# Value products of a hybrid attention trunk: two banks of transposes per run on TensorE

## The chip, the cores and the metric

The kernel runs on one core of a Trainium2 chip. The metric is the device time of one execution in microseconds (us). Before the change the median of three runs is 3219.77 us (3219.07 to 3225.04). TensorE (PE) does the matmuls and the transposes, VectorE (DVE), ScalarE (ACT) and GpSimd (POOL) the elementwise work, and SyncE (SP) issues the DMAs.

## The reference

One layer over 2048 tokens of width 1024 in float32:

- `h = rmsnorm(x)`, and one projection `h @ w_in` that gives the queries, keys and values of four groups of four heads (64 wide): A stick-breaking attention, causal; B native sparse attention with three branches (compressed keys, eight selected blocks of 64 keys, a window of 512), summed by gates; C differential attention, two softmax maps per head, causal; D a window of 128 with sinks.
- Every branch ends in the same product, `o[q, d] = sum over k of P[q, k] * v[k, d]`, with `P` the weights of 128 queries over the keys that they may see, and `v` 64 wide.
- The groups' outputs are normalised, joined (`mix`), multiplied by `w_out` and added to `x`; then `x = x + relu(rmsnorm(x) @ w_up)^2 @ w_down` with a hidden width of 4096, and a last norm.

## The kernel before

**Stages.** The tokens are handled in four chunks of 512. The dense part runs in the order P0 to P3 (projections), then M0 to M3 (`w_out` and the MLP of a chunk); its matmuls write PSUM tiles `pd`, named pdP and pdM in the profile. Each dense product is split into high and low halves of reduced float32, three matmuls for one (`w_hi`, `w_lo`, `T_hi`, `T_lo`, `u_hi`, `u_lo`). Attention runs beside it, chunk by chunk in the order A, C, D, B (`GROUPS`, L34), on blocks of 128 queries. M of a chunk needs the attention of that chunk, through `mix_d` in DRAM.

**One block of attention.** The scores of 128 queries are made on PE into PSUM tiles `z` (three), turned to weights by DVE and ACT in SBUF tiles `row` (seven), and queued by `item` (L873) as a list of blocks: 128 keys for two heads in A, B and D, two times 128 keys of one head in C. A block thus holds up to two 128x128 pieces, for the half `j = 0` and the half `j = 1` of the output.

**Values.** `values` (L878) takes the items in order. It goes over the blocks by two. For each two it transposes up to four pieces of 128x128 on PE (`tr`, profile line L294) into one PSUM bank of tag `t` (two of them), which ACT copies to an SBUF tile `PT` (three of them, `PB`). This is called a bank here. The products of a bank are made one bank later: when the transposes of the next bank have been written, `products` (L931) writes those of the bank before. If there is no further item, or no free `PT`, the pending bank's products are written at once. A product is `mm(o[64*j:64*j+64, 0:128], v, p)`: the 128x64 values are the weights that PE loads, the transposed piece is the moving operand, and the result goes to partitions 0 to 63 or 64 to 127 of the one PSUM tile `o`. All products of an item add up in the same `o`; at the end of the item it is copied out (`oS`). Each product of float32 operands shows as two MATMUL records, so a full bank has eight.

**Order.** The kernel writes its instructions in an order that it works out itself: `run` (L1483) polls ten generators, and each yields either None or a function (`when`) that tells at what modelled time its next PE instruction has its inputs. The first generator in the list whose time has come goes on; `values` stands ahead of `scores`, and `dense` last. The model charges a value product half of its 128 columns (`share=2`). Instructions reach an engine's queue through the tile framework, which is started with `schedule_with_timeline_sim=True` and can move instructions against each other where their data allows it; PE then takes its instructions in the order that results.

Of the kernel before, what the change touches and what calls it, by code (L numbers as in the profile page):

```python
# [30 lines left out]
UNITS = 4  # L31
QB, RB, PB, WB = 4, 7, 3, 3
PD, ZB, TB = 3, 2, 2
GROUPS = "ACDB"  # L34
OFF = S - 128
UO = 2 * (NT - 1)
# [160 lines left out]
class Trunk:  # L197
# [631 lines left out]
    def loads(self):  # L829
        for c in range(NC):  # L830
            for g in GROUPS:
                yield from getattr(self, "loads_" + g)(c, 4 * c, max(0, c - 1))
# [43 lines left out]
        self.vq.append((self.pa, blocks, v, o, fin, first, last, rel))  # L876

    def values(self):  # L878
        prev = None
        while True:  # L880
            while not self.vq:
                if prev:
                    yield from self.products(*prev)
                    prev = None
                    continue
                if "scores" in self.over:
                    self.over.add("values")
                    return
                yield None
            pa, blocks, keys, obox, fin, first, last, rel = self.vq.pop(0)  # L890
            vt = []
            for k in keys:
                while isinstance(k, tuple) and k not in self.kq:
                    if prev:
                        yield from self.products(*prev)
                        prev = None
                    yield None
                vt.append(self.kq[k] if isinstance(k, tuple) else k)
            blocks = blocks(*vt)
            nb = len(blocks)  # L900
            end = [max(b for b in range(nb) if len(blocks[b][0]) > j) if len(blocks[0][0]) > j else -1
                   for j in range(2)]
            for g in range(0, nb, 2):
                bl = blocks[g:g + 2]
                if self.res["PT"].free == 0 and prev:
                    yield from self.products(*prev)
                    prev = None
                yield from self.res["PT"].take()
                yield self.when([p for P, _ in bl for p in P], "t", TB)
                self.pa = pa  # L910
                ps = self.tt()
                pt = self.tile(self.at, [128, 4, 128], F32, "PT", PB)
                n = 0
                for a, (P, _) in enumerate(bl):
                    for j in range(len(P)):
                        self.tr(ps[:, 2 * a + j, :], P[j])
                        n = 2 * a + j + 1
                self.evac(pt[:, :n], ps[:, :n])
                fl = g + 2 >= nb
                if fl and rel:  # L920
                    rel()
                ops = []
                for a, (P, v) in enumerate(bl):
                    for j in range(len(P)):
                        ops.append((j, v[j], pt[:, 2 * a + j, :], first and g + a == 0, last and g + a == end[j]))
                new = (pa, obox, pt, ops, first and g == 0, fin if fl else None)
                if prev:
                    yield from self.products(*prev)
                prev = new

    def products(self, pa, obox, pt, ops, first, fin):  # L931
        yield self.when([pt] + [v for _, v, _, _, _ in ops], "o" if first else None, 1)
        self.pa = pa
        if first:
            obox.append(self.ot())
        o = obox[0]
        for j, v, p, st, sp in ops:
            self.mm(o[64 * j:64 * j + 64, 0:128], v, p, st, sp, share=2)
        self.res["PT"].give()
        if fin:  # L940
            yield from fin(o)

# [30 lines left out]
    def scores(self):  # L973
# [4 lines left out]
        for c in range(NC):  # L978
            for g in GROUPS:
                if g == "D":  # L980
# [587 lines left out]
```

## Time and profile before

| | us |
|---|---|
| median of three runs | 3219.77 |
| profiled execution | 3224.61 |
| span of the profiled execution | 3222.9 |
| PE busy | 3128.8 (97%) |
| DVE busy | 2063.7 (64%) |
| ACT busy | 1776.0 (55%) |

The span reaches from the first to the last instruction; the profiled execution's own time is 1.7 us longer. A time of the timeline is counted from the start of the span. Busy time of PE is the union of its instructions' recorded durations; matmuls overlap in the array, so that the recorded duration of one (0.40 us for 128x512) is longer than the step from one start to the next (0.23 us).

### The profile page before, as it was taken

The numbers are of one execution on the slowest core, as the hardware profiler recorded it, in microseconds if no ns is written. First come the engines' busy times: TensorE is split into PE (matmuls) and PEld (weight loads), VectorE is DVE, ScalarE is ACT, GpSimd is POOL, SyncE is SP. The second block draws the span as 40 slices with busy tenths as digits, with TensorE's granted clock in tenths as the row PEclk, the third lists the DMA queues.
The fourth block names the chain that finished last, engine by engine and source line by source line (L and its number), as shares of the span: only waits on it lengthen the run. The fifth ranks groups of instructions, "written<-read, shape, count | busy, mean of one in ns | idle before, by whom it ended". The sixth has DMA issues, their size and how long they took to land.

```text
span 3222.9 us, 51242 instructions
## 1 busy us (share of the span) xinstructions
PE 3128.8 (97%) x19152; PEld 2510.3 (78%) x19152; DVE 2063.7 (64%) x4278; ACT 1776.0 (55%) x3459; POOL 714.2 (22%) x479
## 2 busy tenths in 40 slices
PE   7999999999999999999999999999999999999998
PEld 6887877878877777778877677778777777888886
DVE  4774668645668877666658887777655554545545
ACT  4764667545667755555657775565555543333333
POOL 3042312323212122232211122233212112310000
PEclk9999999999999999999999999999999999999999
DMA  7777555664133343364232333444522222423332
GB/s 213 193 193 206 160 160 148 191 176 134 57 97 87 100 110 105 97 164 121 61 100 68 99 95 88 110 117 134 141 63 83 65 61 74 149 81 97 92 98 85
DMA packets 456649, 376.53 MB, mean 117 GB/s; under 512 B 127056, under 2 KB 405712, under 8 KB 454736
## 3 DMA queue, kind: packets, MB, share of 16 engines
q1 hardware_dynamic: 456400, 373.26, 42.0%
q8 instruction: 151, 2.47, 0.3%
q14 instruction: 98, 0.80, 0.1%
HBM read 319.59 MB, written 53.58 MB: 116 GB/s over the span
## 4 chain that ended last, share of the span: by engine, by line
PE 77%; DVE 9%; ACT 5%; DMA 4%; issue 2%; SPq 1%; POOL 1%; DVEq 0%; POOLq 0%; ACTq 0%
PE pdM L290 43%; PE pdP L290 11%; DVE row L116 7%; PE tB L294 4%; PE oB L290 4%; PE zB L290 4%; ACT row L116 4%; PE oC L290 2%; PE zC L290 2%; PE tC L294 2%; SPq L246 1%; PE oA L290 1%; DVE acc L116 1%; PE tA L294 1%; PE zA L290 1%
## 5 line engine op out<-in xcount | busy, mean ns | idle before, releaser
L116 POOL TENSOR_TENSOR w_lo<-raw,w_hi 128x1024 fp32r<-128x1024 f32 (+1 forms) x188 | 469.4, 2501 | 1248.9 <-ACT w_hi L116 1105.4
L116 ACT ACTIVATE w_hi<-raw 128x1024 fp32r<-128x1024 f32 (+2 forms) x376 | 388.2, 1047 | 499.4 <-PE pdM L290 309.5
L116 DVE TENSOR_TENSOR acc<-acc,pdM 128x512 f32<-128x512 f32 (+1 forms) x576 | 370.3, 654 | 193.5 <-PE pdM L290 182.0
L290 PE MATMUL pdM<-T_lo,w_hi 128*128 128x512 f32 (+1 forms) x1088 | 419.6, 386 | 4.4 <-POOL T_lo L116 4.4
L290 PE MATMUL pdM<-T_hi,w_hi 128*128 128x512 f32 (+1 forms) x1088 | 419.5, 387 | 3.8 <-DVE nx L116 2.2
L290 PE MATMUL pdM<-T_hi,w_lo 128*128 128x512 f32 (+1 forms) x1088 | 420.8, 387 | 0.0
L290 PE MATMUL pdM<-w_hi,u_hi 128*128 128x512 f32 x1024 | 405.5, 403 | 11.6 <-DVE acc L116 8.4
L290 PE MATMUL pdM<-w_hi,u_lo 128*128 128x512 f32 x1024 | 405.2, 396 | 3.9 <-DVE u_lo L116 3.9
L290 PE MATMUL pdM<-w_lo,u_hi 128*128 128x512 f32 x1024 | 404.7, 396 | 0.0
L116 DVE TENSOR_TENSOR w_lo<-raw,w_hi 128x1024 fp32r<-128x1024 f32 (+1 forms) x188 | 241.2, 1290 | 214.5 <-ACT w_hi L116 206.0
L116 ACT ACTIVATE row<-row 128x1024 f32<-128x1024 f32 (+7 forms) x292 | 229.0, 801 | 118.5 <-DVE row L116 115.8
L290 PEld LDWEIGHTS pdM<-T_lo,w_hi 128*128 128x128 f32 x1088 | 206.5, 190 | 45.9 <-POOL T_lo L116 4.9
L290 PEld LDWEIGHTS pdM<-T_hi,w_hi 128*128 128x128 f32 x1088 | 206.0, 190 | 45.3 <-DVE nx L116 2.5
L116 ACT ACTIVATE PT<-tB 128x512 f32<-128x512 f32 (+1 forms) x260 | 135.9, 532 | 189.4 <-PE tB L294 186.7
L290 PEld LDWEIGHTS pdM<-T_hi,w_lo 128*128 128x128 f32 x1088 | 206.4, 190 | 42.1 <-issue 1.0
L290 PEld LDWEIGHTS pdM<-w_hi,u_hi 128*128 128x128 f32 x1024 | 193.2, 189 | 58.0 <-DVE acc L116 13.2
L290 PEld LDWEIGHTS pdM<-w_hi,u_lo 128*128 128x128 f32 x1024 | 193.7, 189 | 42.7 <-DVE u_lo L116 5.3
L290 PEld LDWEIGHTS pdM<-w_lo,u_hi 128*128 128x128 f32 x1024 | 193.6, 189 | 41.4 <-issue 1.2
L116 ACT ACTIVATE row<-row,c_mn 128x1024 f32<-128x1024 f32 (+4 forms) x192 | 171.6, 896 | 85.6 <-DVE c_mn L116 84.4
L290 PE MATMUL pdP<-T_hi,w_lo 128*128 128x512 f32 x480 | 194.1, 404 | 3.7 <-DVE w_lo L116 3.7
L290 PE MATMUL pdP<-T_lo,w_hi 128*128 128x512 f32 x480 | 193.4, 403 | 0.0
L290 PE MATMUL pdP<-T_hi,w_hi 128*128 128x512 f32 x480 | 192.7, 401 | 0.0
(209 smaller groups left out, 6604.8 us busy)
## 6 DMA issues: line engine op xcount, KB each, us to landing
raw<-in_w_up_dram SPq DMA_DIRECT2D x128, 512.0 KB, 4.1
raw<-in_w_down_dram SPq DMA_DIRECT2D x128, 512.0 KB, 3.6
raw<-in_w_in_dram SPq DMA_DIRECT2D x72, 512.0 KB, 4.9
acc<-in_x_dram SPq DMA_DIRECT2D x32, 512.0 KB, 4.3
raw<-in_w_out_dram SPq DMA_DIRECT2D x32, 512.0 KB, 4.4
qst<-qk_qA SPq DMA_DIRECT2D x64, 128.0 KB, 3.5
qst<-qk_qC SPq DMA_DIRECT2D x128, 64.0 KB, 2.6
qst<-qk_qD SPq DMA_DIRECT2D x64, 128.0 KB, 3.4
```

The source lines that it names most:

```text
L116: return f(*a, **k)
L246: self.nc.sync.dma_start(dst, src)
L290: self.nc.tensor.matmul(out, a, b, start=start, stop=stop, **k)
L294: self.nc.tensor.transpose(out, a, self.ident[:a.shape[0], :a.shape[0]])
```

## The change

`values` collects up to two pending banks of the same item in a list (`run`) and hands the list to `products` when the transposes of a third bank have been written, when the item ends and the next item's first transposes have been written, or when there is nothing else to do. `products` then writes the products of all banks in the list one after the other, with one `when` ahead of them that asks for all their inputs. The list is gone through backwards: the bank transposed last comes first. The flags for the first and the last matmul of a sum are set for the run as a whole. The number of transposes, copies and products stays as it is.

```diff
+RUN = 2
...
     def values(self):
-        prev = None
+        run = []
...
-                new = (pa, obox, pt, ops, first and g == 0, fin if fl else None)
-                if prev:
-                    yield from self.products(*prev)
-                prev = new
-
-    def products(self, pa, obox, pt, ops, first, fin):
-        yield self.when([pt] + [v for _, v, _, _, _ in ops], "o" if first else None, 1)
+                if run and (len(run) == RUN or run[-1][-2]):
+                    yield from self.products(run)
+                run.append((pa, obox, pt, ops, first and g == 0, fl, fin if fl else None))
+
+    def products(self, run):
+
+        pa, obox, _, _, first, _, _ = run[0]
+        yield self.when([x for r in run for x in [r[2]] + [v for _, v, _, _, _ in r[3]]], "o" if first else None, 1)
         self.pa = pa
         if first:
             obox.append(self.ot())
         o = obox[0]
-        for j, v, p, st, sp in ops:
-            self.mm(o[64 * j:64 * j + 64, 0:128], v, p, st, sp, share=2)
-        self.res["PT"].give()
+
+        ops = [x for r in run[::-1] for x in r[3]]
+        of = [[n for n, x in enumerate(ops) if x[0] == j] for j in range(2)]
+        starts = [n[0] if any(ops[i][3] for i in n) else -1 for n in of]
+        stops = [n[-1] if any(ops[i][4] for i in n) else -1 for n in of]
+        for n, (j, v, p, _, _) in enumerate(ops):
+            self.mm(o[64 * j:64 * j + 64, 0:128], v, p, n == starts[j], n == stops[j], share=2)
+        self.res["PT"].give(len(run))
+        fin = run[-1][-1]
+        run.clear()
```

The other places that wrote the pending bank (`if prev: yield from self.products(*prev)`) now write the pending run in the same way.

## Rows read from the trace of the kernel before

**Rows 1.** The page's first part: busy time, share of the span and instructions of each engine; and the granted clock in 40 slices.

```profile
PE 3128.8 (97%) x19152; PEld 2510.3 (78%) x19152; DVE 2063.7 (64%) x4278; ACT 1776.0 (55%) x3459; POOL 714.2 (22%) x479
PEclk9999999999999999999999999999999999999999
```

**Rows 2.** Busy time by stretch: stretch, its length, then busy us and count of instructions of PE, PEld, DVE, ACT and POOL, the granted clock, the DMA share and GB/s.

```profile
0.00:100.00 100.00, 82.49 (x469) 71.41 (x470) 49.68 (x99) 48.47 (x93) 28.47 (x51) 0.98 0.73 214
...
1800.00:1900.00 100.00, 95.51 (x566) 72.40 (x567) 86.47 (x96) 77.65 (x123) 14.05 (x6) 0.98 0.29 76
...
2500.00:2600.00 100.00, 100.00 (x614) 77.94 (x612) 57.84 (x127) 52.19 (x99) 17.27 (x8) 1.00 0.20 60
```

**Rows 3.** The chain of waits at its end, merged: start, duration, what it was.

```profile
2706.24 66.86 PE pdM L290 x290
...
2863.62 345.87 PE pdM L290 x1523
```

**Rows 4.** Groups of instructions of PE by line, operation, tile and form: count, busy us and mean ns of one, then the idle time ahead of them and what ended it. The value products.

```profile
L290 PE MATMUL oB<-PT,v 128*64 128x128 f32 x1648 | 137.6, 285 | 0.0
L290 PE MATMUL oC<-PT,v 128*64 128x128 f32 x1088 | 99.4, 289 | 0.2 <-ACT PT L116 0.2
L290 PE MATMUL oA<-PT,v 128*64 128x128 f32 x1088 | 93.2, 287 | 1.8 <-ACT PT L116 1.7
L290 PE MATMUL oD<-PT,v 128*64 128x128 f32 x248 | 22.0, 286 | 0.0
L290 PE MATMUL oB<-PT,vcn 128*64 128x128 f32 x128 | 16.2, 298 | 0.0
```

**Rows 5.** The timeline of PE around a run of one bank between dense matmuls: start, duration, instruction and count.

```profile
2046.48 0.40 PE L290 MATMUL pdM<-T_lo,w_hi 128*128 128x512 f32 x1
2046.71 0.39 PE L290 MATMUL pdM<-T_hi,w_lo 128*128 128x512 f32 x1
2047.04 0.66 PE L290 MATMUL oC<-PT,v 128*64 128x128 f32 x8
2047.62 0.50 PE L290 MATMUL pdM<-T_hi,w_hi 128*128 128x512 f32 x1
2047.96 0.39 PE L290 MATMUL pdM<-T_lo,w_hi 128*128 128x512 f32 x1
```

**Rows 6.** The same around two banks whose products happen to stand one behind the other.

```profile
1151.20 0.39 PE L290 MATMUL pdM<-w_lo,u_hi 128*128 128x512 f32 x1
1151.52 1.09 PE L290 MATMUL oC<-PT,v 128*64 128x128 f32 x16
1152.54 0.50 PE L290 MATMUL pdM<-w_hi,u_hi 128*128 128x512 f32 x1
1152.87 0.40 PE L290 MATMUL pdM<-w_hi,u_lo 128*128 128x512 f32 x1
```

**Rows 7.** The timeline of PE where transposes and products take turns.

```profile
1673.59 1.09 PE L290 MATMUL oB<-PT,v 128*64 128x128 f32 x16
1674.61 0.66 PE L294 MATMUL tB<-ident,row 128*128 128x128 f32 x4
1675.20 0.66 PE L290 MATMUL oB<-PT,v 128*64 128x128 f32 x8
1675.78 0.66 PE L294 MATMUL tB<-ident,row 128*128 128x128 f32 x4
```

**Rows 8.** The timeline of PE around eight transposes between dense matmuls.

```profile
1292.25 0.39 PE L290 MATMUL pdM<-T_lo,w_hi 128*128 128x512 f32 x1
1292.48 1.03 PE L294 MATMUL tC<-ident,row 128*128 128x128 f32 x8
1293.27 0.48 PE L290 MATMUL pdM<-T_hi,w_lo 128*128 128x512 f32 x1
1293.59 0.40 PE L290 MATMUL pdM<-T_hi,w_hi 128*128 128x512 f32 x1
```

**Rows 9.** The timeline of PE: the first and the last of the 587 stretches in which nothing but value products follow each other.

```profile
87.89 0.44 PE L290 MATMUL oA<-PT,v 128*64 128x128 f32 x4
...
2693.15 1.09 PE L290 MATMUL oB<-PT,v 128*64 128x128 f32 x16
```

**Rows 10.** Who waited for what, PE alone: total us, times, longest.

```profile
PE oA L290 <- ACT PT L116: 1.7, 5, 0.7
...
PE oC L290 <- ACT PT L116: 0.2, 1, 0.2
```

**Rows 11.** The timeline of all engines: a copy to PT, and the products that come after it.

```profile
1602.49 0.57 ACT L116 ACTIVATE PT<-tB 128x512 f32<-128x512 f32 x1
...
1605.11 0.66 PE L290 MATMUL oB<-PT,v 128*64 128x128 f32 x8
```

**Rows 12.** The timeline of PE where the products of one bank are not in one piece.

```profile
1128.23 0.43 PE L290 MATMUL oA<-PT,v 128*64 128x128 f32 x2
1128.74 0.50 PE L290 MATMUL zC<-kst,qst 128*128 128x512 f32 x1
1129.17 0.65 PE L290 MATMUL oA<-PT,v 128*64 128x128 f32 x6
```

**Rows 13.** Groups of instructions of ACT by form: the copies to PT of a full bank in A.

```profile
L116 ACT ACTIVATE PT<-tA 128x512 f32<-128x512 f32 x128 | 75.7, 596 | 11.8 <-PE tA L294 11.8
```

More of the change, by code (lines that the diff above doesn't have):

```diff
@@ L878, in values @@
     def values(self):
-        prev = None
+        run = []
         while True:
             while not self.vq:
-                if prev:
-                    yield from self.products(*prev)
-                    prev = None
+                if run:
+                    yield from self.products(run)
                     continue
@@ L893, in values @@
                 while isinstance(k, tuple) and k not in self.kq:
-                    if prev:
-                        yield from self.products(*prev)
-                        prev = None
+                    if run:
+                        yield from self.products(run)
                     yield None
@@ L904, in values @@
                 bl = blocks[g:g + 2]
-                if self.res["PT"].free == 0 and prev:
-                    yield from self.products(*prev)
-                    prev = None
+                if self.res["PT"].free == 0 and run:
+                    yield from self.products(run)
                 yield from self.res["PT"].take()
@@ L925, in values @@
                         ops.append((j, v[j], pt[:, 2 * a + j, :], first and g + a == 0, last and g + a == end[j]))
-                new = (pa, obox, pt, ops, first and g == 0, fin if fl else None)
-                if prev:
-                    yield from self.products(*prev)
-                prev = new
-    def products(self, pa, obox, pt, ops, first, fin):
-        yield self.when([pt] + [v for _, v, _, _, _ in ops], "o" if first else None, 1)
+                if run and (len(run) == RUN or run[-1][-2]):
+                    yield from self.products(run)
+                run.append((pa, obox, pt, ops, first and g == 0, fl, fin if fl else None))
+    def products(self, run):
+        pa, obox, _, _, first, _, _ = run[0]
+        yield self.when([x for r in run for x in [r[2]] + [v for _, v, _, _, _ in r[3]]], "o" if first else None, 1)
         self.pa = pa
```

## The prediction

> **What bounds the kernel now.** I read the page's first part, then the busy times by stretch, then who waited for whom, then the timeline of PE instruction by instruction. The first part [rows 1] says PE: 97% of the span, at a clock granted in full almost throughout, with DVE at 64% and ACT at 55%. The idle rest of PE is 3222.9 - 3128.8 = 94.1 us, of which 100 - 82.5 = 17.5 us fall into the first 100 us, before attention works [rows 2]. From there on PE idles in small pieces: nothing in 2500 to 2600 us, 4.5 us in 1800 to 1900 us, where DVE is at its fullest, 86% [rows 2]. Nor does the end of attention hold up the dense part: the last value product starts at 2693.15 us [rows 9], and the chain of waits shows dense matmuls of the chunk before still running from 2706.24 us for 66.9 us; the last uninterrupted stretch begins at 2863.62 us [rows 3]. So the time is the sum of what PE does, in whatever order, and an edit is worth what it takes off PE.
>
> A second look is needed at what "busy" hides. The groups of value products show no idle time ahead of them (0.0 to 1.8 us for over a thousand instructions each) and 368 us of busy time in all [rows 4], so by this view they cost what their number costs, and the change, which keeps the number, would save nothing. The starts in the timeline say otherwise. Dense matmuls of 512 columns start 0.23 us apart; but from the last one ahead of a run of products to the run it is 0.33 us, and from the first one behind it to the second 0.34 us [rows 5]. Each run of products thus delays its neighbours, and the recorded durations cover that up.
>
> The Trainium skill (Perfetto Trace Analysis, section Tensor Engine Instruction) says that the profiler takes the start of a PE instruction from the engine but computes the end from its size. By the busy rows the sum below would be zero, by the starts it is what follows; I go by the starts.
>
> **The change part by part.**
>
> *Fewer runs.* First the price of one run. From the dense matmul ahead of it to the second one behind it a run of eight takes 2047.96 - 2046.71 = 1.25 us [rows 5], one of sixteen, two banks that chance put side by side, 1152.87 - 1151.20 = 1.67 us [rows 6]. The eight more products add 0.42 us, and what is left of the first is 1.25 - 0.42 - 2 x 0.23 = 0.37 us: the price of beginning and ending a run among dense matmuls. Among transposes: four transposes and eight products take 1675.78 - 1674.61 = 1.17 us [rows 7]. Eight transposes among dense matmuls take 1293.59 - 1292.25 = 1.34 us, less two steps of 0.23 us 0.88 us, so 0.11 us each [rows 8]; four are 0.44 us. The price is 1.17 - 0.44 - 0.42 = 0.31 us. Of the 587 stretches in which the trace shows products alone [rows 9], I count 367 that are followed by a transpose. Weighted so, (367 x 0.31 + 220 x 0.37) / 587 = 0.33 us. All runs together cost about 194 us, 6% of the time.
>
> Then the number of runs. A bank is two blocks of an item, so the loops give it. A has two pairs of heads and 16 query blocks i of i + 1 blocks (from i = 8 on two items, the second of eight): 144 banks. C has four heads and half as many blocks: 160. B has 32 compressed items of one bank, 84 banks of windows and 144 of selected keys: 260. D has 32. That is 596, and 587 stretches fit it: some banks are joined by chance [rows 6], some are cut in two [rows 12]. In runs of two within an item A needs 80, C 96, B 32 + 56 + 80 = 168, D 32: 376, that is 220 fewer. Not all of these are a gain. In the trace 39 joined banks sit in stretches of more than eight; the new order would have joined most of them anyway, so 220 - 39 = 181 is the low end. The new order will also have chance neighbours, across items. I take 190, nearer the low end. 190 x 0.33 = 63 us. Both ends: 181 x 0.31 = 56 us and 220 x 0.37 = 81 us.
>
> *The bank transposed last comes first.* This costs no instruction. Its copy to PT takes 0.60 us [rows 13], and all products of the run now stand behind it. Before, between a bank's transposes and its products stood the run of the bank before and the next bank's transposes; now only the latter. The cover goes down by one run, 0.58 us [rows 5]. In the trace the cover is usually long: the copy that ends at 1602.49 + 0.57 = 1603.06 us is used at 1605.11 us, 2.05 us later [rows 11], and all waits of value products for a copy come to 1.7 + 0.2 = 1.9 us in 6 times [rows 10]. Bounds: 0 below, and above a whole copy for each of the 220 merged runs, 220 x 0.60 = 132 us. The rows are far nearer to 0; I take 0 here and let it stand as a rival.
>
> *Longer hold of buffers.* Two of three PT tiles are held until a run is over, so the copies of the next two banks wait for it; the two PSUM banks of tag t let a third bank's transposes go only when the first is copied. Dense matmuls and scores fill such time, and they have somewhere to go until 2773 us [rows 3]. If attention had no filler, each pair of banks would show some 0.5 us of idle PE; the rows give no sign of that, so 0, with the next item as the upper end.
>
> *What is late next.* When PE takes 2% less for the same work, DVE and ACT have 2% less time beside it. From 1800 to 1900 us DVE is at 86% and PE loses 4.5 us [rows 2]; there the saving may be eaten in part. The 64 merges in A, where this lies, are worth 64 x 0.33 = 21 us at most. I take off a third of that, 7 us, and nothing elsewhere.
>
> Sum: 63 - 7 = 56 us. The profiled execution took 3224.61 us, so 3168.6 us; it lies 4.84 us above the median of 3219.77 us, and the same subtraction there gives 3164 us, 1.7% less.
>
> **The rivals.**
>
> *Half is eaten.* PE takes its instructions in an order fixed beforehand. If the removed time is mostly where another engine is just in time, waits grow. For it: 94.1 us of PE idle are already there [rows 1], in over 30 kinds of waits. Against it: in stretches like 2500 to 2600 us PE doesn't idle at all, with DVE at 58% and ACT at 52% [rows 2]. With half of 63 us: 3219.8 - 31 = 3189 us.
>
> *The run waits for its first product (slower).* The place is the first matmul of each run, which asks for the copy made last. PE takes matmuls in order, so everything behind it waits as well, also dense matmuls that are ready. With a whole copy per merged run, 132 us less the 63 us: 3219.8 + 69 = 3289 us. It decides from 63 / 220 = 0.29 us of waiting per merged run. Against it: a cover of 2 us [rows 11] and 1.9 us of such waits in the whole trace [rows 10], where losing 0.58 us of cover turns few into waits.
>
> The Trainium skill (TensorE: Matmul & The Clock Gate, Part 3, section The mechanism) has matmuls start and end strictly in program order; only loads of weights are drawn ahead. That is the rule that speaks against putting the newest bank first; the trace of before agrees in so far as the products' few waits show as idle time of PE.
>
> *The runs don't come out whole.* The framework may put other matmuls between two products, as it did where a score cuts one bank's products into two and six [rows 12]. If most runs of sixteen were cut once, the number of stretches would stay near 587 and the time near 3220 us. Against it: 24 stretches of sixteen came out whole with no help, and banks cut like this are some 30 of 596.
>
> **How the numbers follow.** The sum as it stands: 0.68, with a range of its own of 3140 (nearly 81 us less) to 3178 us (42 us less). Half is eaten: 0.20. Runs cut: 0.07. Waits for the first product: 0.05. The range of 8 in 10 goes from 3142 us to 3198 us: it holds the first case but for its edges, and most of the second. Times within 0.2% (6.4 us, about what can be told from no change here) come from the runs that are cut: 0.06. Slower by more: the waiting rival and a remainder of the third, 0.05. Faster: 0.89.
>
> **What would show it.** Right: stretches of sixteen products dominate, each 1.02 us from its first start to the next instruction, and the number of stretches is near 400; counts of products and transposes stay as in rows 4; steps of 0.33 us ahead of products are fewer in the same proportion; PE's idle time grows by no more than some 10 us. Wrong: idle time of PE ahead of the o tiles put down to ACT's PT (the waiting rival: it would have to reach tens of us); 550 stretches or more (cut runs); idle time ahead of dense matmuls and scores put down to DVE and ACT that grows by 30 us (half eaten). The prediction fails as a whole if the price of a run is not for beginning and ending it but for each bank, against which the sixteen speak [rows 6].

## The result, and the profile after

The changed kernel takes 3187.41 us (median of five, 3182.32 to 3192.22) against 3219.63 us before: a ratio of 0.9897, 95% interval 0.9882 to 0.9911, 32 us or 1.0% less. Forecast were 3164 us with 3142 to 3198 us as the range: the direction and the range held, the gain is a little over half of the 56 us.

The two profiled executions lie at opposite ends of their runs (3224.61 us is near the highest of five before, 3225.04 us; 3182.32 us is the lowest after), so their traces differ by 42.3 us. The accounts below are of the traces; where two kernels are called faster or slower than each other, the medians say so.

One correction to the description ahead of the prediction: there are two PSUM tiles `z` for scores, not three (`ZB` is 2; the three is `PD`, the dense sums).

The first part of the page after the change (compare [rows 1]; span 3180.6 us):

```profile
PE 3074.8 (97%) x19152; PEld 2515.3 (79%) x19152; DVE 2068.3 (65%) x4278; ACT 1772.9 (56%) x3459; POOL 710.3 (22%) x479
PEclk9999999999999999999999999999999999999999
```

The counts are those of before on every engine. PE's busy time is 54.0 us less, and its idle time 3180.6 - 3074.8 = 105.8 us, 11.7 us more. The groups of value products, to set beside [rows 4]:

```profile
L291 PE MATMUL oB<-PT,v 128*64 128x128 f32 x1648 | 121.5, 281 | 0.0
L291 PE MATMUL oC<-PT,v 128*64 128x128 f32 x1088 | 87.2, 285 | 0.0
L291 PE MATMUL oA<-PT,v 128*64 128x128 f32 x1088 | 79.6, 282 | 1.7 <-DMA v<-nat_vA 1.7
L291 PE MATMUL oD<-PT,v 128*64 128x128 f32 x248 | 22.5, 287 | 0.0
```

As many instructions of nearly the same length, but A, B and C, whose banks were joined, are busy 42 us less together, while D, with one bank per item, is not. No product waits for ACT's PT any more. The timeline of PE where transposes and products take turns, as in [rows 7]:

```profile
1691.02 0.60 PE L295 MATMUL tB<-ident,row 128*128 128x128 f32 x4
1691.55 1.09 PE L291 MATMUL oB<-PT,v 128*64 128x128 f32 x16
1692.57 0.66 PE L295 MATMUL tB<-ident,row 128*128 128x128 f32 x4
```

Sixteen products take 1.02 us to the next transposes, where two runs of eight took 2 x 0.58 us [rows 7] besides the cost at the second's beginning. The first and the last of the stretches of products, of which there are now 398 (587 in [rows 9]); 147 of them hold sixteen (24 before):

```profile
85.86 0.44 PE L291 MATMUL oA<-PT,v 128*64 128x128 f32 x4
...
2687.57 1.09 PE L291 MATMUL oB<-PT,v 128*64 128x128 f32 x16
```

Where the gain went is in the waits of PE. The list of who waited for what (total us, times, longest) after the change, its largest entries in A and C:

```profile
PE zC L291 <- DVE c_mn L117: 12.6, 13, 3.1
...
PE zA L291 <- ACT row L117: 6.3, 8, 2.1
...
PE tA L295 <- ACT oS L117: 4.7, 2, 3.7
...
PE tA L295 <- ACT row L117: 3.7, 2, 2.6
...
PE tC L295 <- ACT oS L117: 3.0, 3, 2.1
...
PE zC L291 <- DMA row<-in_cmp_w_k_dram: 2.8, 3, 1.7
PE tC L295 <- DVE row L117: 2.7, 1, 2.7
...
PE tA L295 <- ACT PT L117: 2.1, 3, 0.8
```

The largest such entries of the kernel before:

```profile
PE zA L290 <- ACT row L116: 6.9, 7, 2.4
PE zC L290 <- DVE c_mn L116: 5.3, 4, 3.0
...
PE zC L290 <- DMA row<-in_cmp_w_k_dram: 3.4, 2, 2.9
...
PE tC L294 <- ACT oS L116: 1.8, 2, 1.1
...
PE tA L294 <- ACT row L116: 1.8, 2, 1.3
```

Summed over all releasers, PE's idle time ahead of transposes and scores in A and C is 40.4 us (tA 11.2, tC 5.8, zA 6.4, zC 17.0), against 20.0 us before (2.0, 1.8, 7.0, 9.2). So it is transposes and the scores of C that wait longer, not the scores of A; ahead of all other instructions PE's idle time fell by about 9 us. By stretches (PE, PEld, DVE, ACT, POOL busy, clock, DMA share, GB/s), after the change, beside [rows 2]:

```profile
1800.00:1900.00 100.00, 94.44 (x583) 72.82 (x582) 80.48 (x87) 74.34 (x120) 16.16 (x6) 1.00 0.36 95
1900.00:2000.00 100.00, 91.04 (x543) 70.77 (x544) 80.22 (x115) 65.49 (x104) 24.75 (x12) 0.98 0.36 96
2500.00:2600.00 100.00, 100.00 (x619) 78.89 (x618) 54.76 (x124) 51.42 (x97) 17.48 (x9) 1.00 0.22 65
```

In B (2500 to 2600 us) PE still doesn't idle; at the end of A and the start of C in the last chunk (1900 to 2000 us) it idles 9 us in 100, where the same stretch had 4 us before:

```profile
1900.00:2000.00 100.00, 95.76 (x553) 72.40 (x552) 75.95 (x134) 62.27 (x103) 23.78 (x12) 0.97 0.40 107
```

An account of the two traces, from the starts of all PE instructions: for each stretch of products I took the time from the instruction ahead of it to the second one behind it, less the undisturbed steps of what lies in it. Over all stretches this is 208.8 us before and 142.1 us after, 0.36 us for a stretch in both. All other time beyond undisturbed steps is 99.2 us before and 122.9 us after: 11 us more of shown idle time, and some 12 us that show as no idle time, perhaps waits so short that the recorded duration of the instruction ahead covers them. -66.7 + 23.7 = -43.0 us is the difference from PE's first to its last start.

The granted clock isn't behind the 24 us. Between PE's first and last start it is at its lower level of 1.2 GHz for 58 us before and 55 us after the change, each time beside a single wait of PE of 1.1 to 3.7 us. What PE loses there against undisturbed steps, idle time aside, is 25 us in both traces. Between executions, though, the clock matters: over 56 executions of the kernel before, the mean granted clock lies between 0.988 and 0.992, and 0.001 less goes with some 2 us more. The means of the kernels below differ by up to 0.006, so a difference of a few us between two of them can be the clock's.

### The profile page after: what moved, and what is told of

It is laid out like the page before. It is cut to its first block, busy times and chain, and to the rows that moved or that the text cites. A ratio compares the mean times of both kernels' runs of the same rounds, so it can differ in the third digit from the quotient of the medians.

```text
span 3180.6 us, 51156 instructions
## 1 busy us (share of the span) xinstructions
PE 3074.8 (97%) x19152; PEld 2515.3 (79%) x19152; DVE 2068.3 (65%) x4278; ACT 1772.9 (56%) x3459; POOL 710.3 (22%) x479
## 4 chain that ended last, share of the span: by engine, by line
PE 75%; DVE 12%; ACT 6%; DMA 3%; issue 2%; POOL 1%; SPq 1%; DVEq 0%; POOLq 0%; ACTq 0%
PE pdM L291 40%; PE pdP L291 13%; DVE row L117 8%; PE zB L291 4%; PE tB L295 4%; PE oB L291 4%; ACT row L117 4%; PE zC L291 2%; PE oC L291 2%; PE tC L295 2%; DVE acc L117 1%; ACT w_hi L117 1%; DMA raw<-in_w_in_dram 1%; PE tA L295 1%; DMA raw<-in_w_out_dram 1%
## 5 line engine op out<-in xcount | busy, mean ns | idle before, releaser
L117 DVE TENSOR_TENSOR w_lo<-raw,w_hi 128x1024 fp32r<-128x1024 f32 (+1 forms) x188 | 249.3, 1333 | 220.3 <-ACT w_hi L117 211.9
```

Source lines behind the costliest of these rows:

```text
L117: return f(*a, **k)
```

## The experiments

The open question was where the 24 us of waits come from, and whether the price of a run is what I took it for. **Theory 1**: in A and C another engine sets the pace, so PE time is worth less there. **Theory 2**: the merged runs themselves bring it, by holding PT tiles or waiting for the newest copy. **Theory 3**: the written order is worked out without the price of a run. **Theory 4** came later: that price, which no model holds, had served as slack against DVE and ACT.

### Where the shortfall lies: runs of two in some groups alone

```diff
-                if run and (len(run) == RUN or run[-1][-2]):
+                if run and (len(run) == (RUN if run[-1][0][0] in "BD" else 1) or run[-1][-2]):
```

> Runs of two banks in groups B and D alone (D has one bank per item, so in effect B): 92 of the 220 merges. Theory 1, the price of a run is paid back in full where DVE has room and the shortfall lies in A and C: about 92 x 190/220 = 79 stretches fewer, 79 x 0.32 = 25 us saved, so about 3194 us. Theory 2, every merged run loses a like part of its gain (waiting for the newest copy, buffers held longer): 32/60 of that, 13 us, so about 3206 us.

The mirror image, with `"AC"` in the place of `"BD"`:

> Runs of two banks in groups A and C alone: 128 of the 220 merges. Theory 1: some 110 stretches fewer are worth 35 us, but all of the shortfall of the whole change (about 25 us) lies here, so only some 10 us are left: about 3209 us. Theory 2: the same share is lost as anywhere, 19 us saved, about 3201 us.

B alone: 3198.41 us, ratio 0.9934 (0.9922 to 0.9947), 21.4 us less with 515 stretches, 72 fewer; at 0.33 us these are worth 24 us, so nine tenths came off. A and C alone: 3214.45 us, ratio 0.9985 (0.9976 to 0.9994), 5.3 us less with 469 stretches, 118 fewer and worth 39 us, so a seventh came off. The sum, 27 us, is near the 32 us of the whole. The shortfall lies in A and C, as theory 1 has it, and the gain there is smaller still than the 10 us that it forecast (3209 us). Some 4 us of the 21 go with a higher granted clock, 0.993 against 0.991 before; with A and C alone it is 0.990.

The account of the two traces, made in the same way, tells where it went. With runs in A and C alone the stretches take 46 us less than before, and everything else 32 us more; in B alone they take 21 us less, and everything else 6 us less. So in A and C the price came off in full, and most of it came back outside the runs. (By the medians even more did: the trace with A and C alone is of the shortest of eleven executions, that of before of one nearly as long as the longest of five.) PE's waits in the kernel with runs in A and C alone:

```profile
PE zC L291 <- DVE c_mn L117: 8.7, 8, 2.4
...
PE tA L295 <- ACT PT L117: 5.0, 6, 2.2
PE zA L291 <- ACT row L117: 4.2, 7, 1.2
...
PE tA L295 <- ACT on L117: 3.7, 3, 3.0
```

Transposes of A and scores of C wait here too, as after the whole change.

### The backward order

```diff
-        ops = [x for r in run[::-1] for x in r[3]]
+        ops = [x for r in run for x in r[3]]
```

> The changed kernel with the banks of a run in the order in which they were transposed. If the backward order is what keeps the runs whole, the stretches of sixteen fall well under 147, the number of stretches rises from 398 to 450 or more, and the time rises by at least (450 - 398) x 0.32 = 17 us over 3187 us. If the planner's one wait ahead of a run already sees to that, the stretches stay near 400 and the time within 5 us of 3187 us. If waiting for the newest copy first is what costs the shortfall, the time falls under 3180 us.

3227.3 us, ratio 1.0024 (1.0015 to 1.0032): slower than the kernel before, and 40 us slower than with the backward order. There are 536 stretches, and 77 of sixteen in the place of 147. The timeline of PE in this kernel, and ACT's copies at that time:

```profile
2465.81 0.66 PE L291 MATMUL oB<-PT,v 128*64 128x128 f32 x8
2466.40 0.50 PE L291 MATMUL pdM<-T_hi,w_lo 128*128 128x512 f32 x1
2466.83 0.66 PE L291 MATMUL oB<-PT,v 128*64 128x128 f32 x8
```

```profile
2462.93 0.60 ACT L117 ACTIVATE PT<-tB 128x512 f32<-128x512 f32 x1 [0.21 <-PE tB L295]
2465.07 1.06 ACT L117 ACTIVATE w_hi<-raw 128x1024 fp32r<-128x1024 f32 x1 [1.54 <-PE pdM L291]
2466.04 0.58 ACT L117 ACTIVATE PT<-tB 128x512 f32<-128x512 f32 x1
```

My reading of this place: the older bank's products go as soon as its copy is there, and the framework puts a dense matmul between, since the newer copy is still to come. The products of one sum keep their order, so with the newest first none can start before the last copy, and then nothing is left to part them. I had held the backward order to cost nothing; it is what makes the change work. The 51 stretches that are saved here would be worth 17 us; instead the time rose by 7.5 us. The account of the trace puts this at the stretches: they take 210 us, as much as before though they are fewer, 0.39 us each, and PE's idle time in them is 21.0 us in the place of 11.5 us; everything else is as before.

### The planner told of the price

```diff
         self.res["PT"].give(len(run))
+        self.plan.pe += 0.32
```

> The changed kernel, but its own model of PE is told of 0.32 us for each run of products. Theory 3, the shortfall comes from a written order that is worked out without that price and asks other engines' results too early: waits of PE shrink and the time falls by 10 us or more under 3187 us. Theories 1 and 2: within 5 us of 3187 us.

3186.59 us, ratio 0.9896 (0.9882 to 0.9909), 404 stretches: no difference from the change itself. Theory 3 falls.

### What PE time is worth in A and in B

```diff
-                            self.dot(z[:, :w], w, q, (j, qs), k[j], p0, not diag)
+                            self.mm(z[:, :w], q[0][:, j, qs], k[j][:, p0:p0 + w], True, not diag)
```

> The kernel before, which leaves out the second (low) half of every score matmul of group A: 112 matmuls of 512 columns, 16 of 384, 16 of 256 and 16 of 128 less on PE, by their steps 112 x 0.23 + 16 x (0.17 + 0.12 + 0.06) = 31 us. Nothing else is touched, and no product is moved. Theory 1 (in A another engine sets the pace, so PE time is worth less there): less than half of it comes off, 3205 to 3220 us. Theory 2 (PE time is worth the same everywhere, and the shortfall belongs to the runs themselves): 3219.6 - 31 = 3189 us, within 6 us.

The same in the loop over the selected keys of B; the low half of these scores is left out:

```diff
-                        self.dot(z[:, :w], w, q[pr], (j, qs), k_sel, p0)
+                        self.mm(z[:, :w], q[pr][0][:, j, qs], k_sel[:, p0:p0 + w], True, True)
```

> The kernel before, which leaves out the second (low) half of every score matmul over the selected keys of group B: the same number and sizes of matmuls as in A, 31 us of PE. Both theories: nearly all of it comes off, 3189 us within 6 us. If little comes off here too, PE isn't the bound in B either, and theory 1 is wrong in its place.

A: 3197.92 us, ratio 0.993 (0.9916 to 0.9943), 23.2 us of 31. B: 3195.67 us, ratio 0.9919 (0.9906 to 0.9933), 25.5 us of 31. For A this misses theory 1, which forecast 3205 us or more, and theory 2's 3189 us within 6 us too, the latter by little: PE time in A is worth three quarters, in B four fifths, and the two intervals overlap (B's kernel had the higher granted clock, 0.993 against 0.990). B's time is at the upper edge of what was forecast for it. Two things follow. In these two trials a fifth to a quarter of the time that was taken off PE did not come off the whole. And that PE is held up by another engine in A can't by itself explain why only a seventh of the price came off in A and C.

### The price, taken away

```diff
-RUN = 2
+RUN = 1
...
-            self.mm(o[64 * j:64 * j + 64, 0:128], v, p, n == starts[j], n == stops[j], share=2)
+            self.mm(o[:, 0:128], self.ident, p, n == 0 and starts[0] >= 0, n == len(ops) - 1 and stops[0] >= 0)
```

> Runs of one bank as before the change, but each product loads a 128x128 weight (the identity) in the place of the 64 columns of values and writes all 128 partitions; the output is not the attention's. If the price of a run belongs to the 64-column weights, the step from a dense matmul into a run falls from 0.33 to 0.23 us and from a transpose from 0.20 to 0.11 us, the step after a run to its own, and the price of 0.31 to 0.37 us is gone; the products lose their side by side halves and take up to 0.86 us per bank in the place of 0.42 us: about 3220 + 525 x 0.43 - 190 = 3256 us. If it belongs to any change between transposes and products, the steps stay and the time is about 3446 us.

The timeline of PE around a run of eight in this kernel, to set beside [rows 5]:

```profile
1048.49 0.39 PE L291 MATMUL pdM<-w_hi,u_hi 128*128 128x512 f32 x1
1048.72 0.39 PE L291 MATMUL pdM<-w_hi,u_lo 128*128 128x512 f32 x1
1048.95 1.05 PE L291 MATMUL oA<-PT,ident 128*128 128x128 f32 x8
1049.75 0.48 PE L291 MATMUL pdM<-w_lo,u_hi 128*128 128x512 f32 x1
1050.07 0.40 PE L291 MATMUL pdM<-w_hi,u_hi 128*128 128x512 f32 x1
```

The step into the run is 0.23 us as between any two dense matmuls (0.33 us in [rows 5]). From the dense matmul ahead to the second one behind it takes 1.35 us; less 2 x 0.23 us, 0.89 us is left for eight products, 0.11 us each, the same as a transpose. Nothing is left over: the price belongs to the change between 64-column and 128-column weights. (The edit changes the width of the weights and the half of the output that a product writes together; it can't tell the two apart.) The time is 3301.82 us in its only execution, 46 us more than the 3256 us expected and far from the 3446 us of the other reading; 525 x (0.89 - 0.42) - 587 x 0.33 = 53 us more than 3220 us gives 3273 us, so 29 us of it aren't in this sum; part of them are products in A that now wait for their copies, 8.9 us:

```profile
L291 PE MATMUL oA<-PT,ident 128*128 128x128 f32 x1088 | 149.6, 278 | 9.2 <-ACT PT L117 8.9
```

The Trainium skill (TensorEngine Tiling (Array Packing), section Key Properties) says that changing the tiling mode, as against changing the tile within a mode, drains the engine. This run and [rows 5] fit it; the page has no figure, and the rows give 0.31 to 0.37 us for going into a mode and out again.

### More room for scores, more slack, more PT tiles

```diff
-PD, ZB, TB = 3, 2, 2
+PD, ZB, TB = 2, 3, 2
```

> The changed kernel with three PSUM banks for scores and two for dense sums (2 and 3 as it stands). Theory 1: the waits of scores for DVE in A and C (16 us of zC's and 6 us of zA's in the trace) shrink, and the time falls by 5 to 15 us under 3187 us, unless dense groups now wait for their sums' reader. Theory 2: no gain, 3187 us or more.

3222.72 us, ratio 1.0007 (0.9997 to 1.0017): the whole gain is gone. PE's waits show both sides:

```profile
PE pdM L295 <- DVE nx L117: 23.2, 9, 7.0
...
PE pdM L291 <- DVE acc L117: 10.6, 10, 2.1
...
PE zC L291 <- DVE c_mn L117: 5.9, 4, 2.4
```

The scores of C wait less for DVE's c_mn (5.9 for 12.6 us) and less in all (12.3 for 17.0 us), but the dense part, with one sum less, waits more: 80 us in all for 48 us. The scores of A wait more as well (12.3 for 6.4 us), so the scores of A and C together wait no less. Some 6 us of the loss go with a lower granted clock, 0.987. Whether a third z tile would help if it cost the dense part nothing, this run doesn't show.

```diff
-    HOP, MARGIN = 0.15, 0.1
+    HOP, MARGIN = 0.15, 0.6
```

> The changed kernel, with the margin by which its written order lets attention's PE work follow its modelled inputs raised from 0.1 to 0.6 us. Theory 4: the price of the runs, which no model holds, had served as slack, so that PE came late enough to what DVE and ACT make in A and C; with the price gone PE comes too early. Then slack written into the order brings the lost part back: waits of tA, tC and zC shrink, and the time is 5 to 15 us under 3187 us. Theory 2 (longer hold of buffers in A and C): no gain, 3185 us or more.

> The kernel before with the same margin of 0.6 us. Theory 4: it has its slack already, so nothing is gained: 3215 to 3226 us. If it gains as much as the changed kernel does, the margin is worth something by itself and says nothing on the change.

After: 3206.56 us, ratio 0.9958 (0.9946 to 0.997). Before: 3238.13 us, ratio 1.0052 (1.004 to 1.0064). The margin costs 19 us with the change and 18 us without. Theory 4 asked for a gain with the change alone; there is none, so this gives it no support.

```diff
-QB, RB, PB, WB = 4, 7, 3, 3
+QB, RB, PB, WB = 4, 7, 5, 3
...
-        if c == 0:
-            self.last_gain = self.const.tile([128, D], F32, name="last_gain")
-            self.ld(self.last_gain, dap(self.norm_final, 0, [[0, 128], [1, D]]))
...
+            if last:
+                yield from self.res["nx"].take()
+                self.last_gain = self.tile(dn, [128, D], F32, "nx", 2)
+                self.ld(self.last_gain, dap(self.norm_final, 0, [[0, 128], [1, D]]))
...
+            if last:
+                self.res["nx"].give()
```

> The changed kernel with five PT tiles in the place of three; the room comes from the last norm's gain, which is loaded into an nx tile at the end of each chunk in the place of a tile of its own. Theory 2 (copies and transposes wait until a run gives its PT tiles back): the waits of tA, tC and zC go back towards the 10 us of before (37 us in the changed kernel's trace), and the time is 10 to 20 us under 3187 us. Theory 4: the waits stay, 3187 us within 6 us.

3201.0 us, ratio 0.9941 (0.9929 to 0.9953), 14 us slower than with three tiles. The nx tile that the norm's gain now takes is part of that, so the time by itself says little; the waits do:

```profile
PE zC L291 <- DVE c_mn L117: 12.7, 13, 3.3
...
PE zA L291 <- ACT row L117: 9.2, 10, 3.1
...
PE tA L295 <- ACT PT L117: 4.5, 5, 1.6
```

They didn't shrink: ahead of transposes and scores in A and C PE idles 49.6 us, against 40.4 us with three tiles. As far as this run shows, the hold of PT tiles isn't what makes A and C wait. The two PSUM banks for transposes, which the runs also press on, stayed two in every run.

### Three banks in B

B had paid its price back, so the version that should beat both has longer runs there.

```diff
-                if run and (len(run) == RUN or run[-1][-2]):
+                if run and (len(run) == (3 if run[-1][0][0] == "B" else RUN) or run[-1][-2]):
```

> The changed kernel with runs of up to three banks in group B and two elsewhere; PT stays at three tiles, so a run of three is written before the next bank's transposes. B's runs by the loops fall from 168 to 124. If a run's price of 0.31 to 0.37 us is paid back in B as it was at two banks (21 us for 72 stretches), some 40 stretches fewer bring 10 to 14 us: about 3175 us. If a run of three, with no transposes of a next bank ahead of it, makes PE wait for the copy, waits of oB for ACT's PT show up and the time is 3187 us or more.

3154.51 us (3152.5 to 3162.33), ratio 0.9795 (0.978 to 0.9811): 65 us less than before and 33 us less than the change. The first part of its page (span 3160.6 us; this execution is the longest of its five):

```profile
PE 3061.2 (97%) x19152; PEld 2513.9 (80%) x19152; DVE 2052.0 (65%) x4278; ACT 1768.6 (56%) x3459; POOL 712.3 (23%) x479
```

There are 361 stretches, 37 fewer than after the change, worth 12 us at 0.33 us. That is what I had asked of it; 33 us is far more. Waits of oB for ACT's PT, the sign of the other outcome, come to 1.4 us. The rule for A and C is that of the change (A has 95 stretches in the place of 84, C 99 in the place of 102), and yet PE's idle time is 3160.6 - 3061.2 = 99.4 us, 6 us under the change, and ahead of transposes and scores in A and C 31.1 us (40.4 us). So part of the waits that the change had brought is not bound to its runs in A and C: another written order has fewer of them.

Not all of the 33 us is explained so. The two traces, of the shortest execution after the change and the longest here, differ by 20 us: 9 us less at the stretches, 11 us less elsewhere. And the mean granted clock of the executions is 0.993, against 0.990 after the change, which goes with some 7 us. Whether fewer waits brought the higher clock, no run shows.

## Why the prediction was right, and where it wasn't

**What bounds the kernel**: right. Time came off as PE was relieved, and the busiest other engines stayed at 65% and 56%. The look past "busy" to the steps between starts was what carried the forecast. The sentence that the busy view would show a saving of zero was too strong: the count of instructions did not change, but the union of their durations did, by 42 us for the products of A, B and C.

**Price of a run**: right. I had 0.31 to 0.37 us; the account of both traces has 0.36 us for each, waits at the runs included, and the full-width kernel shows that it belongs to the width of the weights.

**Number of runs**: right, but with luck: 190 fewer were forecast, 587 - 398 = 189 came, and they came because of the order within the run, which the count did not consider.

**The bank transposed last comes first**: its cost was right, and its use was missed. No product waits for ACT's PT after the change, so the rival that was to be slower fell. That the order keeps the runs whole stood nowhere in my steps; without it there are 536 stretches, and the kernel is slower than before. The rival in which runs don't come out whole is thus real, and the backward order is what excludes it. What I had set against it, 24 stretches that came out whole and some 30 banks that were cut, was no sufficient reason: with the oldest bank first about half of the runs of sixteen were cut in spite of them (77 are left of 147).

**Longer hold of buffers**: 0 was right for the PT tiles, as far as five of them show; for the two PSUM banks no run tests it.

**What is late next**: this term failed. I took off 7 us, a third of the merges in A, because DVE is fullest there. In the traces 23.7 us came back outside the stretches; of PE's idle time, that ahead of transposes and scores in A and C grew by 20 us and the rest fell by 9 us. By the medians it is 190 x 0.33 - 32 = 31 us. C was left out wrongly: 12 of the 20 us are its own. Taking a known 31 us off PE without touching a product gave back 18 to 25%, so from the 63 us some 14 us were to be expected on that ground alone, from whichever group they come. The time is that of the "half is eaten" rival, 3189 us, to which I had given 0.20. Its reason, an order of PE fixed beforehand in which waits grow, fits the rows in part only: its sign was idle time ahead of dense matmuls and scores that grows by 30 us, and what grew was 13 us ahead of transposes and 7 us ahead of scores in A and C, while the dense matmuls' fell by 4 us.

What stays open is the rest, 10 to 17 us, and why with runs in A and C alone the time outside the runs grew by most of what the runs had saved. The runs speak against four causes: that PE time is worth little in A, the number of PT tiles, the planner's ignorance of the price, and too small a margin. The kernel with three banks in B suggests that it hangs on the particular order, which every edit deals anew; I have no run that holds the order fixed and changes the price alone. Since one edit brought 21 us more than its price and another 34 us less, the split between B and the groups A and C may itself be in part such a chance.

## What to carry to other kernels

Where PE is the bound, look at the steps from start to start around each kind of matmul, since the recorded durations hide the time that is lost between kinds; here each change from full-width to half-width weights and back cost a third of a microsecond, and gathering like with like saved it. When a scheduler may reorder, put the operand that is ready last at the head of a chain whose order is kept: then the chain starts late but is not taken apart. In this kernel a fifth to a quarter of a saving on PE, and half of this one, came back as time elsewhere; so measure where it is paid back before extending the edit. Here that pointed to longer runs in one group, which doubled the gain, though more of it came than the price of the runs accounts for.

## What the runs showed of the hardware that I had not expected

Two products with 64 columns of weights into the two halves of the output go side by side: in the trace of before they start in pairs some 7 ns apart, and eight more of them in a run take 0.42 us, eight full-width ones 0.89 us. The half-width form is thus twice as fast within a run, and only its beginning and end are dear. And the price depends little on the neighbour's work: between transposes it is 0.31 us and between dense matmuls 0.37 us. Nor does it grow with the run: over all stretches it is 0.36 us before and after the change.
